# Position 7's native steps are spread over the steps of positions 2 and 3, with nine weight buffers and three shared sum tiles

## The chip, the cores and the metric

The kernel runs on one core of one Trainium2 chip. The metric is device time in microseconds (us). TensorE (PE in the profile) multiplies, PEld are its weight loads, VectorE (DVE) and ScalarE (ACT) do the elementwise work, SP issues the weight loads (DMAs), and each of these queues works in its own fixed order.

## The reference, cut to what matters

Two blocks on 256 tokens of width 1024: first a hybrid layer (state space and attention), then two layers of a conformer kind, the second with a mixture of experts. The change lies in that mixture, at the end of the program:

```
logits = xf @ w_router                      # 256 x 8 experts
top_vals, top_idx = top_k(logits, 2);  gates = softmax(top_vals)
# every expert e, on the tokens sent to it (d_ff = 3584):
y = (silu(x_e @ w1[e]) * (x_e @ w3[e])) @ w2[e] * gate
f = sum of y over each token's two experts
h = layer_norm(alpha * h + f + e_ple, ln2_g, ln2_b)
```

All is float32. Each expert has three weight matrices of 1024 x 3584, 44 MB in all, and all eight are read.

## The kernel before

The experts are sorted by their number of tokens into positions: position 0 is expert 0, and 1 to 7 hold the others, the largest first. Each position has a fixed number of token slots: 128 for 2 and 3, 128 and a further block of 64 (called NE) for 1, 64 for 0, 4 and 5, 32 for 6 and 7. Extra passes for experts that overflow stand behind branches at the end.

An expert's inner width of 3584 is cut into seven steps of 512 (NJ = 7). A step is six loads (units) of 1 MB: four for the up-projection (w1, w3), two for the down-projection (w2). `STEPS` lists the order in which the positions take steps; before, the end is `(1, 5, 6) * 7`, then `(2, 7) * 7`, then `(3,) * 7`, at indices 14 to 34, 35 to 48 and 49 to 55.

There are two kinds of steps. For positions 1, 2 and 3 (`WIDE`) each unit is split in two halves, and each half into a high part `whi`, which ScalarE casts (L305), and a low part `wlo`, which VectorE subtracts (L306); a product is then three matmuls on `whi`, `wlo` and the likewise split tokens (L324 to L326): 48 matmuls for an up-projection and 24 for a down-projection. These are called split steps here. For positions 0, 4, 5, 6 and 7 the raw weights are multiplied directly (native steps: L1583 up, L1612 down), without work for ScalarE and VectorE on the weights.

`passes` runs the loop: for step i it issues the up-projection (`hidden`), then the first half of the down-projection of step i-1 (`down`), then the transposes of step i's result (`later`), then the second half of that down-projection. Here this is called block i. When a position has finished its seventh step its sum is scaled by the gates (`scaled`, tiles `yh`, `yl`) and added to the tokens' rows `hb` one block later (`scatter`); for the last step `last_sums` does so. Positions 2 and 3 keep their sums in PSUM (two `sm` banks); those in `aside` (NE, 4, 5, 6, 7) keep them in an SBUF tile `y`, to which VectorE adds each step's product (L1632). A position's tokens are gathered into `xg` (split) or `xn` (native) shortly before its first step (`gather`).

Loads are issued by SP in order of use, in a ring of raw buffers, 8 KB per partition each: four in `rawp`, three in `raw2`, one in `raw4`, and two in `raw3` that are given up at step 2 (`narrow`), so eight from there on. Up to four units are prepared ahead (`rows_unit`, `ahead`), and the halves of three units are held at once. The order on each engine's queue is set by a scheduler when the program is built. Last, `rows` (called at a step index) builds two rows for the closing layer norm, and `last_norm` writes the result.

Of the kernel before, what the change touches and what calls it, by code (L numbers as in the profile page):

```python
# [8 lines left out]
F32 = mybir.dt.float32  # L9
# [8 lines left out]
P = 128  # L18
D = 1024
# [6 lines left out]
RAW3 = 2  # L26
# [9 lines left out]
NE = 8  # L36
FE = 3584
NJ = FE // 512
# [101 lines left out]
_, C_TRI, C_STRI, C_CAUS, C_SGN, C_IOTA, C_LESS = 0, 128, 256, 384, 512, 513, 641  # L140
# [62 lines left out]
def _steps(order):  # L203

    return [(e, order[:i].count(e)) for i, e in enumerate(order)]


def _moe_order(steps):


    out = []
    for i in range(len(steps) + 1):
        if i < len(steps):
            out += [(steps[i][0], 6 * steps[i][1] + t) for t in ((0, 2, 1, 3) if steps[i][0] in TURNS else range(4))]
        if i:
            out += [(steps[i - 1][0], 6 * steps[i - 1][1] + t) for t in (4, 5)]
    return out
# [2 lines left out]

TURNS = (0, 1, 4, 5, 6, 7)

STEPS = _steps((0, 0, 0, 4, 0, 4, 0, 4, 0, 4, 0, 4, 4, 4) + (1, 5, 6) * NJ + (2, 7) * NJ + (3,) * NJ)

WIDE = (1, 2, 3)

MORE = 5

WHOLE = [a + i for a in (0, 52) for i in (1, 2, 3, 4, 15, 16)]

FIXED = [e for e, _ in _moe_order(STEPS)].index(4)

# [16 lines left out]
class Kern:  # L249
    def __init__(self, tc, ctx, A, nring=(4, 3)):  # L250
# [14 lines left out]
        if "wm" in A:  # L265
            self.srcs += [(A["wm"][0, u], e in WIDE) for e, u in _moe_order(STEPS)[:FIXED]]

# [907 lines left out]
    def moe(self, l, h, hT, out):  # L1175
# [4 lines left out]
        tc, nc, A = self.tc, self.nc, self.A  # L1180
        mm = nc.tensor.matmul
        with ExitStack() as ctx:
            raw2 = ctx.enter_context(tc.tile_pool(name="raw2", bufs=3))
            mp = ctx.enter_context(tc.tile_pool(name="moe", bufs=1))
            self.gat = ctx.enter_context(tc.tile_pool(name="gat", bufs=1))
            self.xgs, self.xns, self.ohs = [], [self.gat] * 2, [self.gat] * 2

            rctx = ctx.enter_context(ExitStack())
            raw3 = rctx.enter_context(tc.tile_pool(name="raw3", bufs=RAW3))
            self.raws = [raw2] * 3 + [raw3] * RAW3 + self.raws  # L1190
            rctx2 = ctx.enter_context(ExitStack())
            rt = rctx2.enter_context(tc.tile_pool(name="rt", bufs=1))
            wrh, wrl = self.wr
# [67 lines left out]
            def choose(dst, src, ind, n):  # L1261
                nc.vector.tensor_mul(eq[:, :n], ind, src[:, None, :].to_broadcast([P, n, NE]))
                nc.vector.tensor_reduce(dst, eq[:, :n], axis=AX.X, op=OP.add)

            whof = rt.tile([P, NE + 1 + MORE], F32, name="whof")
            choose(whof[:, :NE], iota, perm, NE)
# [10 lines left out]
            nc.vector.tensor_tensor(ovf, ovf, caps, op=OP.is_gt)  # L1277
            nc.vector.tensor_reduce(whof[:, NE + MORE:], ovf, axis=AX.X, op=OP.add)
            order = rt.tile([P, NE + 1], F32, name="order")
            choose(order[:, :NE], ovf[:, :NE], self.less, NE)  # L1280
            nc.vector.tensor_reduce(order[:, NE:], ovf[:, :NE], axis=AX.X, op=OP.add)
            ind = rt.tile([P, MORE, NE + 1], F32, name="ind")
            for i in range(MORE):
                nc.vector.scalar_tensor_tensor(ind[:, i], order, float(i), ovf, op0=OP.is_equal, op1=OP.mult)

            def overflowing(dst, src):
# [3 lines left out]
                if dst[1] is not None:  # L1290
                    nc.vector.tensor_sub(some, some, dst[1])
                each = rt.tile([P, MORE, NE + 1], F32, name="each", bufs=2)
                nc.vector.tensor_mul(each, ind, some[:, None, :].to_broadcast([P, MORE, NE + 1]))
                nc.vector.tensor_reduce(dst[0], each, axis=AX.X, op=OP.add)
# [23 lines left out]
            self.raws = [raw4] + self.raws  # L1318
            self.ahead = 3
            self.mp = ctx.enter_context(tc.tile_pool(name="exp", bufs=1, side="right"))  # L1320
            self.xgs, self.xns, self.ohs = [], [self.gat] * 2, [self.gat] * 2

            def narrow():
                self.raws = [p for p in self.raws if p is not raw3]
# [1 line left out]
            def widen():  # L1326
# [7 lines left out]
            self.srcs += [(A["wm"][0, u] if e == 0 else self.wsrc(es[e - 1], u), e in WIDE)  # L1334
                          for e, u in _moe_order(STEPS)[FIXED:]]
            a, b, q = P, P // 2, P // 4
            fin, stats, gb = [], [], []

            def rows():

                for i in range(2):
                    t = self.ya.tile([P, D], F32, name=f"y{5 + i}")
                    for c in range(2):
                        acc = self.bank([P, 4, P], "acc")
                        for k in range(4):
                            at = KD * i + 4 * c + k
                            mm(acc[:, k], self.gb[:, at:at + 1].to_broadcast([P, P]), self.ident, start=True, stop=True)
                        nc.scalar.copy(t[:, 512 * c:512 * c + 512], acc.rearrange("p a b -> p (a b)"))
                    gb.append(t)
                fin.extend(self.ya.tile([P, D], F32, name=n) for n in ("y7", "y8"))  # L1350
                stats.append(self.mp.tile([P, NT, 2, 6], F32, name="stats"))

            def done(sums):
                self.last_norm(r, sums, fin, stats[0], *gb, out)
            self.passes(posp, gatep, STEPS, r, first, [
                {4: [(4, b)]}, {1: [(1, a), (NE, b)], 5: [(5, b)]},
                {6: [(6, q)], 7: [(7, q)]}, {2: [(2, a)]}, {3: [(3, a)]}], (NE, 4, 5, 6, 7), {2: narrow, 3: widen, len(STEPS) - NJ + 2: rows}, done)
            n = nc.values_load(who[0:1, NE + MORE:], min_val=0, max_val=MORE)
            with ExitStack() as some:
                for i in range(MORE):  # L1360
                    some.enter_context(tc.If(n > i))
                    e = nc.sync.value_load(who[0:1, NE + i:NE + i + 1], min_val=0, max_val=NE - 1)
# [97 lines left out]
    def passes(self, pos, gate, steps, r, got, groups, aside=(), events={}, done=None):  # L1460

        todo, left, ys = None, None, {}
        groups = list(groups)
        for i, step in enumerate(steps + [None]):
            new = None
            if i in events:
                events[i]()

            for e, _ in steps[i:i + (3 if i > 5 else 1)]:
                if e not in got:  # L1470
                    got.update(self.gather(gate, groups[0], self.one_hot(pos, groups.pop(0))))
            later = None
            if step:
                e, j = step
                out, later = self.hidden([b[1] for b in got[e]], e in TURNS)
                new = (e, j, out)
            if left:
                self.scatter(left, r)
                left = None
            if not step:  # L1480
                break
            if todo:
                e, j, gs = todo
                if j == 0:
                    ys[e] = [self.ya.tile([P, D], F32, name=f"y{7 if b[0] == 4 else b[0]}") if b[0] in aside else
                             [self.bank([P, 512], "sm") for _ in range(2)] for b in got[e]]
                    ys[e] = [[y[:, :512], y[:, 512:]] if b[0] in aside else y for y, b in zip(ys[e], got[e])]
                here = [b[0] in aside for b in got[e]]
                self.down(ys[e], gs, j, here, (0,))
                later()  # L1490
                self.down(ys[e], gs, j, here, (1,))
                if j == NJ - 1:
                    left = self.scaled(ys[e], got[e])
            else:
                later()
            todo = new
        done(self.last_sums(r, todo, ys, got, aside))
# [180 lines left out]
```

## Time and profile before

| what | us |
|---|---|
| median of 3 runs (lowest, highest) | 1919.47 (1915.2, 1926.11) |
| the profiled execution | 1920.03 |
| its span, first to last instruction | 1918.2 |
| TensorE busy in the span | 1799.3 (94%) |
| VectorE, ScalarE busy | 1156.7 (60%), 845.3 (44%) |
| granted clock of TensorE, mean | 0.977 |

The shares are means over stages with different limits; the span alone doesn't say which engine a stage waits for. The stretches that the change touches are the table's rows from 1549 us to the end: positions 2 and 7 from there to about 1780, position 3 from there to 1900, and the closing norm in the last 18 us.

### The profile page before, as it was taken

The numbers are of one execution on the slowest core, as the hardware profiler recorded it, in microseconds if no ns is written. First come the engines' busy times: TensorE is split into PE (matmuls) and PEld (weight loads), VectorE is DVE, ScalarE is ACT, GpSimd is POOL, SyncE is SP. The second block draws the span as 40 slices with busy tenths as digits, with TensorE's granted clock in tenths as the row PEclk, the third lists the DMA queues.
The fourth block names the chain that finished last, engine by engine and source line by source line (L and its number), as shares of the span: only waits on it lengthen the run. The fifth ranks groups of instructions, "written<-read, shape, count | busy, mean of one in ns | idle before, by whom it ended". The sixth has DMA issues, their size and how long they took to land.

```text
span 1918.2 us, 26708 instructions
## 1 busy us (share of the span) xinstructions
PE 1799.3 (94%) x10242; PEld 1289.8 (67%) x10242; DVE 1156.7 (60%) x2109; ACT 845.3 (44%) x1369; POOL 8.8 (0%) x21
## 2 busy tenths in 40 slices
PE   6999999998998999999799889999999989899996
PEld 6998888897875999887554234444444546656775
DVE  6548899757897655589840014334444465647887
ACT  4756566444473545347411013322333444535674
POOL 0000000000000000000000000000000000000000
PEclk9999999999998999999889999999999999999998
DMA  6543444454534554463449999789999999999992
GB/s 246 195 150 116 154 160 170 168 191 173 218 110 156 187 196 176 175 237 133 162 190 420 421 421 418 318 352 381 384 382 383 371 382 405 421 421 421 353 339 85
DMA packets 82873, 515.17 MB, mean 269 GB/s; under 512 B 8688, under 2 KB 17568, under 8 KB 22960
## 3 DMA queue, kind: packets, MB, share of 16 engines
q1 hardware_dynamic: 69296, 494.57, 65.4%
q10 hardware_dynamic: 13440, 18.80, 3.1%
q8 instruction: 83, 1.36, 0.3%
q14 instruction: 54, 0.44, 0.1%
HBM read 512.24 MB, written 1.10 MB: 268 GB/s over the span
## 4 chain that ended last, share of the span: by engine, by line
PE 79%; DVE 11%; DMA 5%; ACT 2%; issue 2%; DVEq 0%; ACTq 0%
PE acc L325 14%; PE acc L326 14%; PE acc L324 14%; PE acc L1583 12%; DMA raw<-in_wm 5%; DVE wlo L306 4%; PE sm L1612 3%; PE sm L325 3%; PE sm L326 3%; PE sm L324 2%; DVE cv L1024 2%; PE acc L1612 2%; PE tp L1554 1%; ACT whi L305 1%; PE acc L358 1%
## 5 line engine op out<-in xcount | busy, mean ns | idle before, releaser
L306 DVE TENSOR_TENSOR wlo<-raw,whi 128x1024 fp32r<-128x1024 f32 x490 | 583.1, 1219 | 216.7 <-ACT whi L305 215.9
L305 ACT CAST whi<-raw 128x1024 fp32r<-128x1024 f32 x490 | 494.9, 1048 | 170.9 <-PE acc L326 70.7
L1583 PE MATMUL acc<-raw,xn 128*64 128x512 f32 (+1 forms) x1344 | 276.9, 602 | 15.0 <-DMA raw<-in_wm 15.0
L1583 PEld LDWEIGHTS acc<-raw,xn 128*64 128x64 f32 (+1 forms) x1344 | 82.3, 129 | 184.7 <-issue 155.9
L1544 ACT ACTIVATE eg<-acc 128x512 f32<-128x512 f32 x63 | 37.6, 597 | 361.2 <-PE acc L1583 293.3
L324 PE MATMUL acc<-uhi,whi 128*128 128x272 f32 (+1 forms) x576 | 168.4, 293 | 1.4 <-DVE rs_t L382 1.4
L325 PE MATMUL acc<-ulo,whi 128*128 128x272 f32 (+1 forms) x576 | 167.9, 292 | 0.0
L326 PE MATMUL acc<-uhi,wlo 128*128 128x272 f32 (+1 forms) x576 | 166.5, 289 | 0.0
L324 PE MATMUL acc<-hhi,whi 128*128 128x256 f32 x544 | 152.5, 280 | 0.0
L325 PE MATMUL acc<-hlo,whi 128*128 128x256 f32 x544 | 152.2, 280 | 0.0
L326 PE MATMUL acc<-hhi,wlo 128*128 128x256 f32 x544 | 151.7, 279 | 0.0
L325 PE MATMUL acc<-wlo,xg 128*128 128x512 f32 x336 | 135.7, 404 | 6.2 <-DVE wlo L306 6.2
L324 PE MATMUL acc<-whi,xg 128*128 128x512 f32 x336 | 134.5, 400 | 2.3 <-ACT whi L305 2.3
L326 PE MATMUL acc<-whi,xg 128*128 128x512 f32 x336 | 133.9, 399 | 0.0
L324 PEld LDWEIGHTS acc<-uhi,whi 128*128 128x128 f32 x576 | 109.7, 191 | 4.6 <-issue 2.7
L325 PEld LDWEIGHTS acc<-ulo,whi 128*128 128x128 f32 x576 | 109.6, 190 | 1.4 <-issue 1.0
L326 PEld LDWEIGHTS acc<-uhi,wlo 128*128 128x128 f32 x576 | 109.6, 190 | 1.2 <-issue 1.1
L1024 DVE SCALAR_TENSOR_TENSOR cv<-u,cols,cv 128x256 f32<-128x256 f32 x240 | 102.0, 477 | 2.1 <-ACT cv L1022 1.3
L324 PEld LDWEIGHTS acc<-hhi,whi 128*128 128x128 f32 x544 | 102.3, 188 | 0.2
L325 PEld LDWEIGHTS acc<-hlo,whi 128*128 128x128 f32 x544 | 102.1, 188 | 0.1
L326 PEld LDWEIGHTS acc<-hhi,wlo 128*128 128x128 f32 x544 | 101.8, 187 | 0.0
L1612 PE MATMUL sm<-raw,g 128*64 128x512 f32 (+1 forms) x392 | 90.7, 600 | 0.0
(516 smaller groups left out, 2957.6 us busy)
## 6 DMA issues: line engine op xcount, KB each, us to landing
raw<-in_wm SPq DMA_DIRECT2D x336, 1024.0 KB, 10.4
raw<-in_ws SPq DMA_DIRECT2D x131, 1024.0 KB, 4.8
row<-in_rows ACTq DMA_DIRECT2D x9, 512.0 KB, 4.4
seg<-racs ACTq DMA_DIRECT2D x8, 512.0 KB, 4.1
rb<-in_rpb ACTq DMA_DIRECT2D x8, 512.0 KB, 3.4
ck<-rnck ACTq DMA_DIRECT2D x4, 544.0 KB, 5.6
x<-in_x SPq DMA_DIRECT2D x2, 512.0 KB, 5.2
gn<-in_rows ACTq DMA_DIRECT2D x4, 256.0 KB, 3.3
```

What stands on the lines that cost most here:

```text
L305: nc.scalar.copy(hi, x)
L306: nc.vector.tensor_sub(lo, x, hi.bitcast(F32))
L324: nc.tensor.matmul(out, lhi, rhi, start=start, stop=False)
L325: nc.tensor.matmul(out, lhi, rlo, start=False, stop=False)
L326: nc.tensor.matmul(out, llo, rhi, start=False, stop=stop)
L358: self.nc.tensor.matmul(outs[tb], x[2][:, kk, s], w.raw[:, k], start=start, stop=stop)
L1024: nc.vector.scalar_tensor_tensor(cv[:, m], u[:, m, t:t + T], w, cv[:, m], op0=OP.mult, op1=OP.add)
L1544: nc.scalar.activation(t, h[0], AF.Copy if len(h) == 1 else AF.Silu)
L1554: i = nc.tensor.transpose(tp[:, k], h[0][:, k * P:k * P + P], self.ident)
L1583: self.nc.tensor.matmul(h[0][at:at + n], x[0][:, k0 + k + q], w.raw[:, k + q], start=k0 + k == 0, stop=k0 + k + m == KD)
L1612: self.nc.tensor.matmul(out[h:h + s], x[0][:, kx], w.raw[:, k], start=first and k < m, stop=last and k >= n - m)
```

## The change

`STEPS` ends now in `(1, 5, 6) * 7`, then `2, 7`, three times `2, 2, 7`, three times `3, 3, 7`, and `3`; the steps are the same, 56 in number. `raw2` has four buffers instead of three, so the ring holds nine from step 3 on. To make room, the sums of 4 and 6, of 5 and one norm row, and of NE and 7 share the tiles `ya`, `yb`, `yc` (`SUMS`); the first pool holds one `xn` tile instead of two; and the result's rows (`fin`) take turns in the `xg` tiles. `rows` is called at index 52 instead of 51.

```
-STEPS = _steps((0, 0, 0, 4, 0, 4, 0, 4, 0, 4, 0, 4, 4, 4) + (1, 5, 6) * NJ + (2, 7) * NJ + (3,) * NJ)
+STEPS = _steps((0, 0, 0, 4, 0, 4, 0, 4, 0, 4, 0, 4, 4, 4) + (1, 5, 6) * NJ + (2, 7) + (2, 2, 7) * 3 + (3, 3, 7) * 3 + (3,))
...
+SUMS = {2: "b", 4: "a", 5: "b", 6: "a", 7: "c", NE: "c"}
...
-            raw2 = ctx.enter_context(tc.tile_pool(name="raw2", bufs=3))
+            raw2 = ctx.enter_context(tc.tile_pool(name="raw2", bufs=4))
...
-            self.xgs, self.xns, self.ohs = [], [self.gat] * 2, [self.gat] * 2
+            self.xgs, self.xns, self.ohs = [], [self.gat], [self.gat] * 2
...
-            self.raws = [raw2] * 3 + [raw3] * RAW3 + self.raws
+            self.raws = [raw2] * 4 + [raw3] * RAW3 + self.raws
...
-                    t = self.ya.tile([P, D], F32, name=f"y{5 + i}")
+                    t = self.ya.tile([P, D], F32, name="y" + "ab"[i])
...
-                fin.extend(self.ya.tile([P, D], F32, name=n) for n in ("y7", "y8"))
+                fin.extend(self.turn_of(self.xgs, [P, D], "xg", F32) for _ in range(2))
...
-  {2: narrow, 3: widen, len(STEPS) - NJ + 2: rows}
+  {2: narrow, 3: widen, len(STEPS) - 4: rows}
...
-  ys[e] = [self.ya.tile([P, D], F32, name=f"y{7 if b[0] == 4 else b[0]}") if b[0] in aside else
+  ys[e] = [self.ya.tile([P, D], F32, name="y" + SUMS[b[0]]) if b[0] in aside else
```

The new program's lines from L222 on are two higher than before (L324 is L326). Three places of the two orders follow, before first.

TensorE's queue where a split up-projection of position 2 ends and position 7's down-projection (`sm` and `acc` from `raw`, with the transposes `tp` between) follows:

```order
L326 MATMUL acc<-whi,xg 128x512
L1612 MATMUL sm<-raw,g_14281 32x512 x4
L1554 MATMUL tp<-cst,eg 128x128 x4
L1612 MATMUL acc<-raw,g_14281 32x512 x4
L1583 MATMUL acc<-raw,xn 32x512 x16
L324 MATMUL sm<-whi,egs 128x512
```

```order
L1614 MATMUL sm<-raw,g_14025 32x512 x4
L1556 MATMUL tp<-cst,eg 128x128 x4
L1614 MATMUL acc<-raw,g_14025 32x512 x4
L326 MATMUL acc<-whi,xg 128x512
L327 MATMUL acc<-wlo,xg 128x512
```

Behind the native down-projection stood the native up-projection of 7's next step, which uses raw weights; now the up-projection of position 2's next step stands there, whose third row needs a `wlo`.

VectorE's queue around the same place (`eg` is the product of the two gate halves, `egs` the low part of the transposed result, `y_13772` and `yc` the sum of position 7, `g` its gate):

```order
L1551 TENSOR_TENSOR eg<-eg,acc 128x512
L1632 TENSOR_TENSOR y_13772<-y_13772,sm 128x512
L362 TENSOR_TENSOR egs<-tp,egs 128x512
L1632 TENSOR_TENSOR y_13772<-y_13772,acc 128x512
L306 TENSOR_TENSOR wlo<-raw,whi 128x1024 x4
L1597 TENSOR_REDUCE g_14282<-tp 128x256
```

```order
L1553 TENSOR_TENSOR eg<-eg,acc 128x512
L1634 TENSOR_TENSOR yc<-yc,sm 128x512
L364 TENSOR_TENSOR egs<-tp,egs 128x512
L1634 TENSOR_TENSOR yc<-yc,acc 128x512
L308 TENSOR_TENSOR wlo<-raw,whi 128x1024 x10
L1553 TENSOR_TENSOR eg<-eg,acc 128x512
```

Four halves followed the second addition, for the down-projection after a native up-projection; now ten follow it, eight for the split up-projection that is TensorE's next block and two for the down-projection after it.

VectorE's queue at the end of the last block, before the closing norm (`yl` is the low part of a scaled sum, `hb` the tokens' rows):

```order
L306 TENSOR_TENSOR wlo<-raw,whi 128x1024 x2
L362 TENSOR_TENSOR egs<-tp,egs 128x512
L306 TENSOR_TENSOR wlo<-raw,whi 128x1024 x4
L1643 SCALAR_TENSOR_TENSOR yl<-sm,gsl,yh 128x512
L1512 TENSOR_TENSOR hb<-hb,acc 128x512 x2
```

```order
L1634 TENSOR_TENSOR yc<-yc,acc 128x512
L1645 SCALAR_TENSOR_TENSOR yl<-yc,gsl,yh 128x512 x2
L1658 TENSOR_TENSOR hb<-hb,acc 128x512 x2
L308 TENSOR_TENSOR wlo<-raw,whi 128x1024 x2
L1658 TENSOR_TENSOR hb<-hb,acc 128x512
L308 TENSOR_TENSOR wlo<-raw,whi 128x1024 x2
L1658 TENSOR_TENSOR hb<-hb,acc 128x512
L1645 SCALAR_TENSOR_TENSOR yl<-sm,gsl,yh 128x512
```

The last four halves (the last down-projection's weights) stood behind `egs` alone; now they stand behind position 7's last addition, its scaling and its first scatter. On SP one more expert load, the eighth, stands ahead of the reading of `who`, the router's result.

## Rows read from the trace of the kernel before

**Rows 1.** The page's forty slices: busy share of the DMA engines, in tenths.

```profile
DMA  6543444454534554463449999789999999999992
```

**Rows 2.** Table by stretch: length, busy us (instructions) by engine, clock, DMA share, GB/s.

```profile
1048.00:1131.00 83.00, 69.15 (x296) 23.39 (x293) 4.86 (x9) 5.49 (x11) 0.00 (x0) 1.00 1.01 421
1260.00:1500.00 240.00, 233.00 (x1134) 108.90 (x1133) 100.89 (x117) 77.58 (x101) 0.00 (x0) 1.00 0.92 379
1584.88:1614.00 29.12, 26.69 (x129) 17.68 (x128) 16.22 (x17) 14.72 (x19) 0.00 (x0) 0.88 1.00 394
1614.00:1641.89 27.89, 25.45 (x129) 16.63 (x128) 17.20 (x19) 13.27 (x17) 0.00 (x0) 0.94 1.01 422
...
1805.88:1897.00 91.12, 91.12 (x399) 72.15 (x398) 76.70 (x72) 64.54 (x73) 0.00 (x0) 1.00 0.71 266
...
1779.73:1805.90 26.17, 25.10 (x119) 20.44 (x119) 22.44 (x24) 17.09 (x21) 0.00 (x0) 0.93 0.95 365
```

**Rows 3.** TensorE's timeline, blocks of 2 and 7: start, us, instruction, [idle before].

```profile
1598.74 3.62 PE L1583 MATMUL acc<-raw,xn 128*32 128x512 f32 x32
1604.04 0.50 PE L324 MATMUL sm<-whi,egs 128*128 128x512 f32 x1 [1.68 <-ACT whi L305]
1605.30 0.80 PE L325 MATMUL sm<-wlo,egs 128*128 128x512 f32 x1 [0.76 <-DVE wlo L306]
...
1614.01 0.39 PE L324 MATMUL acc<-whi,xg 128*128 128x512 f32 x1
...
1627.88 3.62 PE L1583 MATMUL acc<-raw,xn 128*32 128x512 f32 x32
...
1634.43 0.50 PE L325 MATMUL sm<-wlo,egs 128*128 128x512 f32 x1 [0.76 <-DVE wlo L306]
...
1641.89 0.40 PE L324 MATMUL acc<-whi,xg 128*128 128x512 f32 x1
```

**Rows 4.** ScalarE's timeline after a native up-projection.

```profile
1631.59 0.60 ACT L1544 ACTIVATE eg<-acc 128x512 f32<-128x512 f32 x1 [3.90 <-PE acc L1583]
1632.08 5.77 ACT L305 CAST whi<-raw 128x1024 fp32r<-128x1024 f32 x6
```

**Rows 5.** TensorE's timeline: first products of two blocks of position 3.

```profile
1858.15 0.39 PE L324 MATMUL acc<-whi,xg 128*128 128x512 f32 x1
...
1875.63 0.40 PE L324 MATMUL acc<-whi,xg 128*128 128x512 f32 x1
```

**Rows 6.** TensorE's timeline where position 3 follows the last step of 7.

```profile
1777.43 1.07 PE L1612 MATMUL acc<-raw,g 128*32 128x512 f32 x8
1779.73 0.50 PE L324 MATMUL acc<-whi,xg 128*128 128x512 f32 x1 [1.23 <-ACT whi L305]
1781.30 0.50 PE L325 MATMUL acc<-wlo,xg 128*128 128x512 f32 x1 [1.06 <-DVE wlo L306]
```

**Rows 7.** VectorE's timeline at the same place.

```profile
1778.77 0.68 DVE L1632 TENSOR_TENSOR y<-y,acc 128x512 f32<-128x512 f32 x1
1779.36 0.74 DVE L1643 SCALAR_TENSOR_TENSOR yl<-y,gsl,yh 128x512 fp32r<-128x512 f32 x1
1780.03 2.35 DVE L306 TENSOR_TENSOR wlo<-raw,whi 128x1024 fp32r<-128x1024 f32 x2
```

**Rows 8.** Timelines of VectorE and TensorE near the end.

```profile
1892.06 4.63 DVE L306 TENSOR_TENSOR wlo<-raw,whi 128x1024 fp32r<-128x1024 f32 x4 [0.26 <-ACT whi L305]
...
1899.51 0.40 PE L326 MATMUL sm<-whi,egs 128*128 128x512 f32 x1
```

**Rows 9.** SP's queue from 986 to 1000 us: loads behind the router's result.

```profile
987.55 12.32 SPq L298 DMA_DIRECT2D raw<-in_wm  x4
```

**Rows 10.** Timelines of TensorE and ScalarE: the gather for position 2, the norm rows.

```profile
1514.40 0.67 PE L1433 MATMUL acc<-oh,thi 128*128 128x128 f32 x4
1515.10 3.57 ACT L1438 CAST xg<-acc 128x256 fp32r<-128x256 f32 x8 [1.16 <-PE acc L1433]
...
1802.22 3.29 PE L1347 MATMUL acc<-cst,wr 128*128 128x128 f32 x28
```

More of the change, by code (lines that the diff above doesn't have):

```diff
@@ L1320, in moe @@
             self.mp = ctx.enter_context(tc.tile_pool(name="exp", bufs=1, side="right"))
-            self.xgs, self.xns, self.ohs = [], [self.gat] * 2, [self.gat] * 2
+            self.xgs, self.xns, self.ohs = [], [self.gat], [self.gat] * 2
             def narrow():
@@ L1356, in moe @@
                 {4: [(4, b)]}, {1: [(1, a), (NE, b)], 5: [(5, b)]},
-                {6: [(6, q)], 7: [(7, q)]}, {2: [(2, a)]}, {3: [(3, a)]}], (NE, 4, 5, 6, 7), {2: narrow, 3: widen, len(STEPS) - NJ + 2: rows}, done)
+                {6: [(6, q)], 7: [(7, q)]}, {2: [(2, a)]}, {3: [(3, a)]}], (NE, 4, 5, 6, 7), {2: narrow, 3: widen, len(STEPS) - 4: rows}, done)
             n = nc.values_load(who[0:1, NE + MORE:], min_val=0, max_val=MORE)
```

## The prediction

> **What bounds the kernel now.** I read the page's forty slices first. The loads' share of time stands at 3 to 6 tenths until slice 21 and at 7 to 9 from slice 22 (1007 us) to the last but one: there the kernel streams expert weights [rows 1]. Then a table by stretch, which shows three regimes [rows 2]. While positions 1, 5 and 6 take turns (1260 to 1500) TensorE is busy 233.00 of 240 us and the loads 0.92: TensorE is the bound, narrowly. While 2 and 7 alternate (a pair is 1614.00 to 1641.89) the loads stand at 1.01 and 422 GB/s and TensorE has 2.4 us to spare: the loads are the bound. In the last steps of position 3 TensorE is busy 91.12 of 91.12 us and the loads fall to 0.71. So the change moves cheap TensorE work out of a stretch that is short of loads into one that is short of TensorE. One load is 1.0486 MB; at 421 GB/s that is 2.49 us, a step of six 14.94 us, wherever loads bind.
>
> Third, TensorE's timeline, to price a step. I cut it into blocks as the loop issues them: up-projection of step i, then down-projection of step i-1.
> - Split after native (A): 1614.01 to 1627.88, 13.87 us [rows 3].
> - Native after split (C): 1627.88 to 1641.89, 14.01 us. In it TensorE stops after 32 native products, until the first `whi` (1.68) and then the first `wlo` (0.76) of the next weights are there [rows 3]. ScalarE shows why: its cast of the native result (1631.59) stands ahead of the casts that make `whi` (from 1632.08), so these can't start while the native products run [rows 4].
> - Split after split (B): 1858.15 to 1875.63, 17.48 us, without a wait [rows 5].
>
> A pair A + C has 27.9 us of TensorE with its waits against 29.9 us of loads; an all-split step has 17.5 against 14.9. Spread evenly, the 21 steps of 2, 7 and 3 would need 21 x 14.94 = 314 us of loads and nothing more; the question is what TensorE needs for them in the new order.
>
> **The change part by part.** Steps 37 to 54 become six triples: split, split, native, that is A, B, C. Their work is the same products as before; what counts is where TensorE stands still.
>
> *The new seam.* Between the two split steps of a triple, native down-projection ends, and the next split up-projection follows at once (before, a native up-projection stood there, which needs no split). VectorE's queue now has, behind the second addition into `yc`, all ten `wlo` that follow; the first of them is the one that the next TensorE block starts with. The addition needs the down-projection's last product. So each triple gets a wait: addition, then one `wlo`. Before there is one such place, where 7 is followed by 3 [rows 6, 7]: the native down-projection is issued at 1777.43, the addition runs at 1778.77 for 0.68, a `yl` at 1779.36 for 0.74, the first `wlo` from 1780.03, and TensorE waits 1.23 and then 1.06, 2.29 in all. Without the `yl` (about 0.65 in steady state) the `wlo` ends near 1780.6 and TensorE is some 2.0 us late against an unbroken run. In the first triple the addition is a copy on ScalarE ahead of the casts; I add 0.9 there. Bounds: 0, if the addition came early enough, and 2.9. I take 2.0. Queued behind the waiting `wlo` are the other nine; TensorE uses one half of a load in six products of 0.235 (17.48 over 72 products and four transposes), 1.4 us, and VectorE makes one in 1.16 (4.63 for four), so the delay doesn't grow [rows 5, 8].
>
> *A triple* is then 13.87 + 17.48 + 2.0 + 14.01 = 47.4 us; six are 284.2. Its eighteen loads need 44.9: TensorE, with its waits, becomes the bound, by 2.5 us. The loads' slack lies in the ninth buffer.
>
> *Ninth weight buffer.* One more load is issued ahead of SP's wait for the router's result: eight in that group instead of seven. Before, that load waited until 987.55 [rows 9]; the stretch after it is bound by loads (share 1.01 from 1048 to 1131, TensorE 69 of 83 us) [rows 2], so it shifts by one load: -2.5 us, and the stage of 1, 5, 6 starts that much earlier. Bounds 0 (the buffer comes free no earlier) and -5 (two loads). In that stage TensorE is the bound and the buffer is worth nothing.
>
> *Three sum tiles, one `xn` fewer in the old pool, output rows in the `xg` tiles.* No operation is added. The users of one tile lie far apart: 4 ends before 6 begins, the block NE of position 1 ends before 7 begins, 2's `xg` is unread long before the output. What would cost is a wait of a first write for the last read; there are blocks between each pair. 0.
>
> *Moved work that loses its cover.* Position 3's gather lay in the stretch bound by loads. A gather whose eight copies ScalarE made in one go (3.57 us, from 0.7 after TensorE's start) took TensorE 4.3 us [rows 10]. Now ScalarE has four `whi` (5.77 for six, so 0.96 each [rows 4]) between those copies, and TensorE can be some copies ahead (an estimate, 1.1): 4.3 + 3.8 - 1.1 = 7, of which 2 replace that triple's wait: +5 (2.3, if the `whi` cost nothing, to 8). Position 2's scatter, eight products of 0.235, lies in a triple: +1.9. The norm rows' 32 products, 28 of them in 3.29: +3.7 [rows 10].
>
> *The end.* Position 7 now ends one step before the last, so its sum is scattered just ahead of the last down-projection. VectorE's order there after the last native product: addition 0.68, two `yl` 1.48, two additions into `hb` of the same form 1.36, then four `wlo` (4.63) with another (0.68) between, then TensorE's six products (1.4) and four scatter products (0.95): 11.2, with hand-overs between the engines 12. Bounds: 8.5 if TensorE's 24 + 4 + 8 products run unbroken, 14.
>
> *The sum.* The block at 1584.88 is the first of triple one; before and after are the same up to there but for the -2.5: 1582.4. Plus 284.2 + 0.9 (triples), + 5 + 1.9 + 3.7, + 13.87 (block 55, split after native), + 12: 1904.0. Before, the last down-projection product started at 1899.51 [rows 8] and ended 0.23 later; what follows it is the same. Difference +4.2 us. The profiled execution took 1920.03 us (span 1918.2); the median of the three runs is 1919.47, 0.56 below it. So 1920.03 + 4.2 - 0.56 = 1923.7: I forecast **1924 us, no measurable change**, half a per cent (9.6 us) being about what a measurement of this kernel tells from none.
>
> **TensorE's clock.** In the pairs the granted clock is 0.94, in the first of them 0.88; in the stretch of 1, 5, 6 and in the last steps of 3 it is 1.00 [rows 2]. It fell to its low level (1.2 GHz) after the native step and its wait, and matmuls ran at 0.80 and 0.50 then [rows 3]. C as priced contains one such fall; the C from 1598.74 to 1614.01, with twice the time at the low level, took 15.27, 1.26 more. Without any fall the 24 products and transposes after the wait would take 6.2 instead of 7.5, so a triple 1.2 less. [...]
>
> **The rivals.**
> A. *The loads bind: faster.* The waits overlap with the slack that the interleaving gives, and a triple takes 44.9 us, the time of its loads. Then 6 x 2.5 = 15 us less, 1909 us. For it: 1.01 in all pairs, and the same steps of 3 without any wait in rows 5. Against it: both waits come from the order in the queues, and rows 3, 6 show them while loads were landed or not. 0.2.
> B. *The clock falls twice per triple: slower.* At the seam TensorE does 2.4 us of thin native products, waits 2, and starts a block of 48 dense ones. At the one such place before (1779.73) the clock of the stretch that follows is 0.93 [rows 2]. A fall cost 1.26 above; six, at 1.5 for blocks that are denser, are +9: 1933 us. It decides if TensorE's granted clock in triples is under about 0.93. 0.25.
> C. *The buffer and order do less than they say*: the eighth early load waits as long as before, so the shift of 2.5 us fails, and nothing else changes: 1926. 0.05. The forecast itself, triples of 46 to 48 us, has 0.5.
>
> **How the numbers follow.** The forecast's own range: a triple without a fall of the clock, -7, to a gather at 8 and a tail at 14, +5: 1917 to 1929. Faster by over 0.5% (under 1909.9) is A: 0.2. Slower (over 1929.1) is B and some of the forecast's upper edge: 0.3. Within: 0.5. The low end of the range is A with two early loads and the cheap gather (1909 - 2.5 - 2.7 = 1903.8, taken as 1903), the high end B with the dear gather and tail (1933 + 3 + 2 = 1938).
>
> **What would show it.** (1) At six places, after native down-projection, TensorE waits about 2 us for `wlo`, VectorE's addition into `yc` just ahead; if those waits are under 0.5 us, the seam step is wrong. (2) Triples of 46 to 48 us, with the loads' share 0.93 to 0.98, not 1.01; a share of 1.01 with 44.9 is rival A. (3) The granted clock in the triples: 0.96 is the forecast, below 0.93 rival B. (4) The load at 987.55 issued by 980, and the stage of 1, 5, 6 earlier by 2.5 us. (5) Between the last native product and the last down-projection product 12 us. The forecast is wrong as a whole if triples differ from 47.4 by more than 1.6 us.

## The result, and the profile after

The changed kernel took 1932.94 us (median of 15 runs, 1927.77 to 1943.25), the kernel before 1918.1 us in 15 runs of the same series: 1.0081 of it, 95% interval 1.0067 to 1.0095. It is slower by 0.8%, 15 us. The forecast of 1924 us is 9 us short. The time lies in the whole range that was stated (1903 to 1938) but above the forecast's own (1917 to 1929), and "no measurable change" was wrong. The profiled execution took 1936.5 us; some 5 us of it are a delay ahead of 100 us that e1 and e4 don't have.

A table by stretch of the changed kernel (length, busy us (instructions) by engine, granted clock, DMA share, GB/s): its six triples, each from one split block behind a native one to the next, and the end.

```profile
1590.41:1638.47 48.06, 43.21 (x206) 30.16 (x204) 31.14 (x31) 27.12 (x33) 0.00 (x0) 0.96 0.97 372
1638.47:1685.95 47.48, 43.41 (x205) 30.36 (x204) 32.28 (x33) 25.97 (x31) 0.00 (x0) 0.96 0.98 399
1685.95:1740.69 54.74, 50.56 (x246) 37.15 (x244) 32.96 (x35) 27.83 (x39) 0.00 (x0) 0.91 0.90 358
1740.69:1788.73 48.04, 43.97 (x214) 30.59 (x212) 36.09 (x38) 28.24 (x33) 0.00 (x0) 1.00 0.98 379
1788.73:1842.47 53.74, 49.72 (x238) 34.28 (x237) 32.35 (x33) 28.31 (x35) 0.00 (x0) 0.97 0.98 395
1842.47:1889.99 47.52, 43.45 (x206) 30.31 (x204) 32.32 (x33) 25.97 (x31) 0.00 (x0) 0.96 0.90 347
1889.99:1915.60 25.61, 23.82 (x106) 16.22 (x105) 19.64 (x24) 11.14 (x15) 0.00 (x0) 1.00 0.15 64
```

The plain triples (second, sixth) take 47.5 us. The third holds position 3's gather, the fourth position 2's scatter, the fifth the norm rows. In none is TensorE busy for the whole time, and in none are the loads at the 1.01 that they had in the pairs [rows 2]: neither is the bound, the waits between the engines are. The list of TensorE's waits (engine, line waited for: us in total, times, longest) for 1590.4 to 1916 names them:

```profile
PE sm L326 <- ACT whi L307: 10.0, 6, 1.7
PE sm L327 <- DVE wlo L308: 5.3, 7, 0.8
PE acc L327 <- DVE wlo L308: 4.8, 5, 1.0
PE acc L326 <- ACT whi L307: 4.1, 5, 1.6
```

The first two are in the main the wait behind each native up-projection, known from [rows 3]; the last two stand at the new seam, in five triples (in the third the gather stands there). TensorE's timeline there (start, us, instruction, [idle before]):

```profile
1651.45 1.06 PE L1614 MATMUL acc<-raw,g 128*32 128x512 f32 x8
1653.14 0.49 PE L326 MATMUL acc<-whi,xg 128*128 128x512 f32 x1 [0.62 <-ACT whi L307]
1654.65 0.80 PE L327 MATMUL acc<-wlo,xg 128*128 128x512 f32 x1 [1.02 <-DVE wlo L308]
```

And the queues of ScalarE and VectorE at the same place:

```profile
1644.76 1.99 ACT L307 CAST whi<-raw 128x1024 fp32r<-128x1024 f32 x2
1651.56 0.58 ACT L363 CAST egs<-tp 128x512 fp32r<-128x512 f32 x1 [4.81 <-PE tp L1556]
1652.04 5.79 ACT L307 CAST whi<-raw 128x1024 fp32r<-128x1024 f32 x6
```

```profile
1651.00 0.69 DVE L1634 TENSOR_TENSOR yc<-yc,sm 128x512 f32<-128x512 f32 x1 [0.34 <-PE sm L1614]
1652.18 0.69 DVE L364 TENSOR_TENSOR egs<-tp,egs 128x512 fp32r<-128x512 f32 x1 [0.49 <-ACT egs L363]
1652.79 0.68 DVE L1634 TENSOR_TENSOR yc<-yc,acc 128x512 f32<-128x512 f32 x1
1653.38 6.89 DVE L308 TENSOR_TENSOR wlo<-raw,whi 128x1024 fp32r<-128x1024 f32 x6
```

ScalarE stands still for 4.81 us, because the cast of the split result (`egs`), which needs the transposes, is ahead of the `whi` in its queue; the six casts behind it then run without a wait for a load. VectorE has both additions and its part of `egs` ahead of the first `wlo`. So there are two queue orders at the seam, of which the prediction named VectorE's alone.

A third sort of row is the clock. A native block with its wait in the first triple, the part behind that wait in the fifth, the stretch behind the second triple's seam, and the two split blocks of the second and of the fifth triple:

```profile
1625.99:1638.47 12.48, 10.04 (x62) 5.94 (x61) 7.19 (x7) 8.15 (x10) 0.00 (x0) 1.00 0.95 381
1834.00:1842.40 8.40, 7.63 (x28) 5.92 (x28) 6.91 (x7) 6.25 (x8) 0.00 (x0) 0.80 1.01 412
1653.14:1657.81 4.67, 3.65 (x9) 2.67 (x10) 4.67 (x5) 4.67 (x5) 0.00 (x0) 0.66 1.02 412
1638.47:1673.49 35.02, 33.38 (x145) 24.41 (x143) 25.12 (x26) 17.84 (x21) 0.00 (x0) 0.95 1.01 412
1788.73:1822.23 33.50, 31.87 (x146) 23.23 (x144) 25.12 (x26) 17.84 (x21) 0.00 (x0) 1.00 1.01 421
```

In the first, second and sixth triple the clock falls to its low level once, behind the seam; in the fifth once, behind the native step; in the gather's triple at both places; in the fourth (1.00) not at all. The two split blocks took 35.02 us with a fall and 33.50 without one, so a fall costs 1.5.

### The profile page after: what moved, and what is told of

It reads as the page before. It is cut to its first block, busy times and chain, and to the rows that moved or that the text cites. A ratio compares the mean times of both kernels' runs of the same rounds, so it can differ in the third digit from the quotient of the medians.

```text
span 1934.7 us, 26712 instructions
## 1 busy us (share of the span) xinstructions
PE 1804.6 (93%) x10242; PEld 1292.4 (67%) x10242; DVE 1156.8 (60%) x2109; ACT 844.2 (44%) x1369; POOL 8.8 (0%) x21
## 5 line engine op out<-in xcount | busy, mean ns | idle before, releaser
L326 PE MATMUL acc<-uhi,whi 128*128 128x272 f32 (+1 forms) x576 | 168.8, 293 | 1.3 <-DVE rs_t L384 1.3
L326 PE MATMUL acc<-hhi,whi 128*128 128x256 f32 x544 | 153.1, 281 | 0.0
L326 PE MATMUL acc<-whi,xg 128*128 128x512 f32 x336 | 136.9, 408 | 5.7 <-ACT whi L307 5.2
L328 PE MATMUL acc<-whi,xg 128*128 128x512 f32 x336 | 136.0, 405 | 0.0
L326 PEld LDWEIGHTS acc<-uhi,whi 128*128 128x128 f32 x576 | 110.3, 192 | 4.5 <-issue 2.4
L326 PEld LDWEIGHTS acc<-hhi,whi 128*128 128x128 f32 x544 | 102.3, 188 | 0.2
```

What stands on the lines that cost most here:

```text
L326: nc.tensor.matmul(out, lhi, rhi, start=start, stop=False)
L328: nc.tensor.matmul(out, llo, rhi, start=False, stop=stop)
```

## The experiments

The theory: the changed kernel's loss lies in its triples, where ScalarE's and VectorE's queues put work that waits for TensorE ahead of casts for which TensorE waits. Its rivals: the loads and their ring, the ninth buffer or the shared tiles, and chance in the profiled executions.

**e1, buffers and tiles alone.**

```
-STEPS ... + (2, 7) + (2, 2, 7) * 3 + (3, 3, 7) * 3 + (3,))
+STEPS ... + (2, 7) * NJ + (3,) * NJ)
...
-len(STEPS) - 4: rows
+len(STEPS) - NJ + 2: rows
```

> The changed kernel with the old order of steps (2 and 7 in turn, then 3): only the ninth buffer, the shared tiles and one xn tile fewer are left of the change. Theory 1 (the order of the steps costs the time, through TensorE's waits at its seams): 1 to 2.5 us less than before, about 1916. Theory 2 (the tiles or the buffer cost what the changed kernel's trace shows before 100 us, where it is 5 us late): 1921 to 1924, with the same 5 us early in its trace. Theory 3 (that early delay is chance): as theory 1, and no delay of 5 us before 100 us in this trace.

1916.29 us against 1917.41: ratio 0.9998 (0.9984 to 1.0012). TensorE waits for loads for 13.0 us between 990 and 1140 us against 13.8 before. The buffer and the tiles cost nothing and bring nothing that can be measured. The 5 us ahead of 100 us that the changed kernel's trace shows are not here: chance.

**e2, the order alone.**

```
-raw2 = ctx.enter_context(tc.tile_pool(name="raw2", bufs=4))
+raw2 = ctx.enter_context(tc.tile_pool(name="raw2", bufs=3))
```

> The changed kernel with three buffers in raw2 instead of four: the new order of steps with the old ring of eight. Theory 1: triples of 47.5 us as in the changed kernel, since TensorE's waits and not the loads set them; 1 to 2 us above the changed kernel, about 1934. Theory 2 (the ring): triples of 48.5 us or more, 1940 and above, since loads now bind.

1937.94 us, ratio 1.0115 (1.0096 to 1.0134); plain triples 47.5 us. With the eight buffers it is as slow as the change, or slightly slower; its tiles are those of e1, which cost nothing. So the order of the steps is the cause.

**e3, the first casts ahead of the others.** `behind` opens a scope in which what is issued on ScalarE (0) or VectorE (1) stands behind the cast of the unit with the given number among the next ones, from step 36 on; no operation is added. The main edits:

```
-nc.scalar.activation(t, h[0], AF.Copy if len(h) == 1 else AF.Silu)
+with self.behind(1, (0,) if len(h) == 1 else ()):    # behind the second next unit's whi
+    nc.scalar.activation(t, h[0], AF.Copy if len(h) == 1 else AF.Silu)
...
-self.split(gh, gl, tp)
+with self.behind(0, (0, 1) if self.native else ()):  # behind the next unit's whi and wlo
+    self.split(gh, gl, tp)
...
-nc.vector.tensor_add(y[c], y[c], o[c])
+with self.behind(0, (1,)):                           # behind the next unit's wlo
+    nc.vector.tensor_add(y[c], y[c], o[c])
```

> The changed kernel, but from step 36 on ScalarE's queue has the whi casts of the next split units ahead of the cast of a native result (eg) and of the split result's high part (egs), and VectorE's queue has the first wlo ahead of position 7's additions and of egs; no operation is added or removed. Theory 1 (both waits per triple are an order in these queues: 2.4 us after the native step, 1.7 at the seam): the waits go, triples fall to 44.9 us, where the loads bind (share 1.0), and the triple with the norm rows and the one with the gather lose 5 us or more; 1933 - 6 x 2.6 - 5 = 1912, 1908 to 1918. Theory 2 (the weights were not there in time, the loads or their halves): the waits stay at some 4 us per triple, 1930 to 1935. Of the clock: if its falls follow the waits, the mean granted clock of the triples rises from 0.96 to 0.99 or more; if they follow the thin native products, it stays at 0.96.

1896.65 us, ratio 0.9891 (0.9873 to 0.9909): 21 us below the kernel before and 34 below the changed one (e4). Theory 1, by 11 us more than its range. Its triples by stretch, in order, and the end:

```profile
1581.25:1622.45 41.20, 41.20 (x205) 29.11 (x204) 31.16 (x31) 27.32 (x33) 0.00 (x0) 1.00 1.01 422
1622.45:1664.30 41.85, 41.48 (x205) 29.14 (x204) 32.27 (x33) 25.87 (x30) 0.00 (x0) 1.00 1.01 420
1664.30:1717.12 52.82, 50.98 (x245) 37.98 (x244) 32.88 (x34) 28.98 (x40) 0.00 (x0) 0.90 0.98 405
...
1760.94:1809.32 48.38, 47.77 (x237) 33.10 (x236) 32.18 (x33) 28.24 (x35) 0.00 (x0) 1.00 1.01 421
1809.32:1850.55 41.23, 41.23 (x205) 29.14 (x204) 32.19 (x33) 25.99 (x31) 0.00 (x0) 1.00 1.01 420
1850.55:1876.10 25.55, 23.75 (x106) 16.18 (x105) 20.04 (x24) 11.58 (x14) 0.00 (x0) 1.00 0.31 127
```

A plain triple takes 41.2 to 41.9 us, TensorE busy for all but 0.4 of it at most, without a fall of the clock: the falls of the changed kernel's plain triples went with the waits. That is below the 44.9 of its loads, which I had taken for a floor: the loads run at 1.01 (0.98 in the gather's triple), and the ring's lead pays the difference. ScalarE and VectorE at its second seam show the queues turned round:

```profile
1631.24 1.99 ACT L308 CAST whi<-raw 128x1024 fp32r<-128x1024 f32 x2 [0.51 <-DMA raw<-in_wm]
1635.54 0.59 ACT L371 CAST egs<-tp 128x512 fp32r<-128x512 f32 x1 [2.31 <-PE tp L1567]
```

```profile
1634.57 2.35 DVE L308 TENSOR_TENSOR wlo<-raw,whi 128x1024 fp32r<-128x1024 f32 x2
1636.84 0.68 DVE L1648 TENSOR_TENSOR yc<-yc,sm 128x512 f32<-128x512 f32 x1
```

**e4, the changed kernel again** (no edit).

> The changed kernel once more, for a second trace of it. Theory 1: 1933, the stretch from triple one to the last down-projection product again 325 us long against 315 before, with one fall of the clock in each triple, at the seam or after the native step; and no delay of 5 us before 100 us (chance). Theory 2: the 5 us before 100 us are there again.

1931.08 us, ratio 1.0078 (1.0059 to 1.0097). From triple one to the end of the last down-projection (1581.83 to 1906.93) it took 325.1 us, against 325.0 in the first trace (1590.41 to 1915.37); the early 5 us are absent.

**e5 and e6, the two halves of e3.** e5 has the first of e3's three changes, e6 the other two (and the like for the first step's copies).

> The changed kernel with only one half of e3's edit: ScalarE's cast of a native result stands behind the whi casts of the next two split units; the seam keeps its queue order. Theory 1 (two separate queue orders): the wait after the native step (1.68 and 0.76 us) goes, the seam's (0.62 and 1.02, six times) stays; the triple loses 2.4 to 2.8 us, 44.7 to 45.1, so with the cheaper norm rows 1912 to 1918. If a clock fall follows each wait, one fall of about 1.4 us is left in each triple, now always at the seam. Theory 2 (the seam alone costs what the change lost): hardly faster than the changed kernel, 1926 or more.

> The other half of e3's edit alone: the first casts ahead of position 7's additions and of egs; the wait after the native step stays. Theory 1: the wait at the seam goes (1.64) and the fall of the clock behind it, which comes back after the native step in each triple: the triple loses 2.0 to 3.5 us, 44.0 to 45.5, 1910 to 1918. Theory 2 (the seam alone costs what the change lost): nearly all of e3's gain, 1898 to 1903.

e5: 1909.11 us, ratio 0.994 (0.9921 to 0.9958). e6: 1920.65, 0.9997 (0.9984 to 1.001). The expected times missed, e5 by 3 us below its range, e6 by 3 above; the plain triples came as theory 1 of each expected. The second and last triple of e5:

```profile
1628.97:1673.72 44.75, 43.12 (x205) 30.28 (x204) 32.35 (x33) 25.98 (x31) 0.00 (x0) 0.96 1.01 421
1820.06:1864.81 44.75, 43.11 (x206) 30.28 (x204) 32.35 (x33) 25.97 (x31) 0.00 (x0) 0.96 0.95 363
```

and of e6:

```profile
1633.43:1677.42 43.99, 41.56 (x206) 29.14 (x205) 32.12 (x33) 26.00 (x31) 0.00 (x0) 1.00 1.01 421
1831.85:1875.86 44.01, 41.57 (x206) 29.14 (x205) 32.14 (x33) 25.98 (x31) 0.00 (x0) 1.00 0.94 377
```

From 47.5, e5 takes 2.75 and e6 3.5, so in plain triples the seam weighs more, by the fall of the clock that goes with it: the native wait alone leaves the clock at 1.00 there (it does fall in e6's fourth and fifth triple, 0.96 and 0.97). Over the six triples it is the other way: 299.6 us in the changed kernel, 279.8 in e5, 286.4 in e6, 269.3 in e3. e5 also shortens the triples of the gather and the norm rows (50.3 and 50.4 us; in e6 55.0 and 51.7).

**e7, both halves in the old order of steps.**

```
-STEPS ... + (2, 7) + (2, 2, 7) * 3 + (3, 3, 7) * 3 + (3,))
+STEPS ... + (2, 7) * NJ + (3,) * NJ)
...
-len(STEPS) - 4: rows
+len(STEPS) - NJ + 2: rows
```

> Both halves of e3's edit with the old order of steps (2 and 7 in turn, then 3) and the nine buffers of e1. Theory 1 (the pairs are bound by their loads, share 1.01, so their waits hide): within 3 us of e1, 1912 to 1917, and so the new order is worth 15 us or more once its waits are gone. Theory 2 (the queue order alone makes e3's gain, in any order of steps): 1900 or less.

1909.7 us, ratio 0.9943 (0.9923 to 0.9963), between the theories. From one native block to the next the pairs took 23.6 and 23.5 us while the ring's lead lasted, then 29.5, 31.3 and 30.5, against 29.9 for their twelve loads. In these TensorE waits for loads, and for casts for which ScalarE itself stands waiting for a load (1628.32):

```profile
PE sm L334 <- ACT whi L308: 5.2, 4, 1.7
PE acc L1597 <- DMA raw<-in_wm: 4.9, 5, 1.4
```

```profile
1628.32 1.99 ACT L308 CAST whi<-raw 128x1024 fp32r<-128x1024 f32 x2 [7.55 <-DMA raw<-in_wm]
```

So a DMA share of 1.01 did not mean that TensorE was held by the loads in the first pairs, and did in the later ones. With the casts first, the new order is worth about half a per cent, 10 us (0.9891 of the kernel before in e3, 0.9943 in e7); with the casts as they were it costs 15.

**e8, another order with the casts first.**

```
-STEPS ... + (2, 7) + (2, 2, 7) * 3 + (3, 3, 7) * 3 + (3,))
+STEPS ... + (2, 7) * 3 + (2,) * 4 + (3,) * 3 + (7, 3) * 4)
```

> Both halves of e3's edit and another order of the last 21 steps: 2, 7 three times, 2 four times, 3 three times, then 7, 3 four times, so that the all-split run, in which TensorE falls behind the loads, stands in the middle, and pairs, in which it catches up, at the end. TensorE's own time from the start of the stretch to the last down-projection is worked out to 284 us (7 blocks of 14.0, 6 of 9.7, 6 of 17.5, gather 5, norm rows 4, scatter 2, end 12), e3's took 294; the 19 steps' loads take 284. Theory 1 (after e3 the loads bind in the stretch, and their lead is lost at the end, where the last load lands 18 us before the last product): 1884 to 1892. Theory 2 (the order of steps no longer matters once the waits are gone): 1895 to 1898.

1908.25 us, ratio 0.9937 (0.9918 to 0.9956). Both expectations missed. The pairs outrun the loads by the third (that native up-projection takes 6.86 instead of 3.62 us, with waits for loads), then the all-split run lets the loads' share fall to 0.89 between 1700 and 1760 us. My sum had TensorE's time and the loads' time each in total, and neither in order: the ring's lead is too short for seven steps of one kind.

**e9, the kernel before again** (no edit).

> The kernel before once more, for a second trace of it: how much of the difference of 14 us between the medians (the stretch from triple one to the last down-projection product shows 10.4 of it) is chance of the one execution that was profiled before. Theory 1 (its stretch there was some 3 us longer than usual, by its falls of the clock): the same stretch, 314.9 us in the first trace, takes 310 to 313 here. Theory 2 (the rest lies ahead of the stretch): 314 to 316.

One run, 1914.87 us; theory 1, by 1 us more than its range. The stretch of [rows 2] from 1584.88 to the end of the last down-projection, in the first trace and then in this one:

```profile
1584.88:1899.74 314.86, 296.84 (x1411) 210.55 (x1410) 218.08 (x222) 175.40 (x211) 0.00 (x0) 0.96 0.91 365
```

```profile
1585.77:1894.69 308.92, 290.13 (x1411) 205.14 (x1410) 218.04 (x222) 175.69 (x211) 0.00 (x0) 0.99 0.91 373
```

The same work took 5.9 us less, with the clock at 0.99 instead of 0.96: the trace that the prediction was made from had more falls than this one. e1, which has the same order of steps, took 311.1. The difference to the changed kernel's 325.0 is 10.1 by the first trace and 16.0 by the second; the medians' 14.8 lies between.

**e10, the casts first from step 14 on.**

```
-self.late = done and 36 <= i < len(STEPS) - 1
+self.late = done and 14 <= i < len(STEPS) - 1
```

> e3's edit, from step 14 on instead of step 36: in the stretch of positions 1, 5 and 6 too the first casts stand ahead of the native results' casts and of the additions. Theory 1 (TensorE is the bound there, and its 13 us of waits for whi and wlo between 1131 and 1581 us are such queue orders): 5 to 12 us below e3, 1885 to 1892. Theory 2 (position 1's waits have another cause, or the loads and the later casts take their place): within 3 us of e3, 1894 to 1900.

1887.67 us, ratio 0.9838 (0.9817 to 0.9859): theory 1. TensorE's waits for casts from 1131 us to 1581 in e3 were these, 10.0 us and not the 13 of the expectation:

```profile
PE acc L335 <- DVE wlo L308: 5.1, 7, 1.1
PE sm L335 <- DVE wlo L308: 3.8, 5, 0.8
...
PE acc L334 <- ACT whi L308: 1.1, 2, 0.8
```

In e10 1.8 us of such waits are left between 1131 and 1880.

**e11, the gather and the norm rows moved.**

```
-for e, _ in steps[i:i + (3 if i > 5 else 1)]:
+for e, _ in steps[i:i + (2 if i > 40 else 3 if i > 5 else 1)]:
...
-len(STEPS) - 4: rows
+len(STEPS) - 3: rows
```

> e3 with two more steps moved: position 3's gather is issued one step later (among the split products of the block before its first step, instead of in one piece at a seam), and the norm rows' 32 products one step later (among split products instead of native ones). Theory 1 (both cost more in the changed kernel than was forecast because of what they stand in: the gather's triple took 11.6 us more than the others in e3, the norm rows' triple 7.2): 3 to 8 us below e3, 1888 to 1893, the gather's excess 6 to 9, the norm rows' 4 to 5. Theory 2 (their cost is their own products and copies, wherever they stand): within 2 us of e3.

1893.83 us, ratio 0.9872 (0.9849 to 0.9895), 3 below e3 in the medians, with intervals that overlap. Its third, fifth and sixth triple:

```profile
1662.60:1708.15 45.55, 45.55 (x246) 33.85 (x244) 32.52 (x34) 29.67 (x40) 0.00 (x0) 1.00 1.01 421
...
1752.05:1800.61 48.56, 44.48 (x206) 31.04 (x205) 32.34 (x33) 26.94 (x32) 0.00 (x0) 0.93 1.02 421
1800.61:1847.42 46.81, 45.10 (x237) 32.84 (x236) 32.27 (x33) 28.04 (x35) 0.00 (x0) 1.00 1.01 420
```

The gather's triple falls from 52.8 to 45.6, without a wait and with the clock at 1.00. The norm rows became dearer: 95.4 us for the last two triples against 89.6 in e3, for two reasons. In the fifth triple the native block has lost the row products, and TensorE waits 3.3 us for a `whi` that ScalarE could not cast before its load came, with a fall of the clock (0.93):

```profile
1790.27 1.99 ACT L308 CAST whi<-raw 128x1024 fp32r<-128x1024 f32 x2 [8.19 <-DMA raw<-in_wm]
```

In the sixth it waits 1.7 us for ScalarE's copy of a norm row. So the loads took back part of what the gather had given.

**e12, e10 with the gather of e11.**

> e10 with the gather's part of e11: the first casts ahead of the others from step 14 on, and position 3's gather one step later; the norm rows stay where e10 has them. Theory 1 (the gather's triple gives the 7 us that it gave in e11, since the last load still lands 17 us ahead of the last product in e10, so the loads' lead has room for it): 1879 to 1883. Theory 2 (the loads, at a share of 1.01 in the whole stretch, take the gain back as waits): 1885 to 1889.

1884.29 us (1882.35 to 1887.51), ratio 0.9816 (0.9791 to 0.984). The median lies between the two expectations; the trace speaks for the first, its gather's triple taking 45.5 us, and TensorE waits for no load in the six triples:

```profile
1657.94:1703.48 45.54, 45.54 (x246) 33.84 (x244) 32.50 (x34) 29.51 (x40) 0.00 (x0) 1.00 1.01 421
```

It beats both kernels: 36 us below the kernel before (1920.39 in that series), 1.8%. Against e10 the intervals overlap.

## Why the prediction was right and wrong

The sum was right in the triple's size and wrong in the ninth buffer and in the moved work. The change is measurable: what came is the "slower" to which the forecast gave 0.3.

- *The triple.* Priced at 47.4 us, measured 47.5, with one fall of the clock as priced (0.96). The seam's wait was put at 2.0 us: TensorE waits 0.62 and 1.02, and two split blocks without a fall took 33.50 us in the fifth triple against 31.5 in e3 (1622.45 to 1653.97), 2.0 more. The size was right; the cause was half of it, since ScalarE's queue has its own share, and the 1.23 of [rows 6], put down to VectorE, was such a wait for `whi`. In part the triple's fit is luck: the 14.01 us of C hold a fall behind the native step, but in the plain triples that block took 12.5 us without one, and the fall came at the seam.
- *The ninth buffer: failed.* Forecast -2.5, measured 0 (e1, within 0.2%). The load that had waited until 987.55 [rows 9] was issued at 973.9 in e1, as forecast, but TensorE's waits for loads fell only by 0.8 us. The load after it was issued at 988.5, where the one before it had waited until then; why the one load of lead is not worth its 2.5 us no run shows.
- *Gather and norm rows: mis-sized.* Forecast +5 and +3.7; against the plain triples +7.2 and +6.2. The gather breaks off dense work; the block behind it ran at the low clock for some of its products, and a second fall stands behind that triple's native step (0.91). The 1.1 us that TensorE was to be ahead of the copies stand in no row. The norm rows were hoisted among thin native products. These took 3.64 us alone and 9.9 with the 32 row products between them.
- *The scatter* was sized rightly: forecast +1.9, and the fourth triple's two split blocks (1740.69 to 1776.25) took 35.56 us against 33.50 in the fifth, both without a fall, 2.1 more. That its triple is only 0.5 above the plain ones is the fall that it lacks. With the first triple's copies (0.9 forecast, 0.6 measured) these four make 3 us more than the sum, counted against the plain triples.
- *The end.* 12 us forecast from the last native product to the last down-projection product, 11.4 measured.
- *The base.* The sum was made against one execution whose stretch took 314.9 us; the same kernel took 308.9 in the second. By the stretch alone the forecast (321.6) was 3.4 short of 325.0. The buffer's 2.5 and these 3.4 leave some 3 of the 9 us by which 1924 missed; they fit a base that was some 3 us too long, as far as the traces bound it, but that share is not measured by itself.
- *Rival A* (loads bind, 44.9 per triple) didn't come; e3 shows that it needed the waits gone, and that the loads are not a floor for a triple while the ring has a lead. *Rival B* gave the time, 1933, without its mechanism: it wanted two falls of the clock per triple and a granted clock below 0.93, and there was one, at 0.96; only the gather's triple had two. *Rival C* was right that the buffer gives nothing, but not in its reason: the load did come early.

## What to carry to other kernels

Before reordering steps, read what stands ahead of each cast or copy in its engine's queue at the new neighbours: here an order that put a result's cast before the next weights' cost more than the balance of loads gave, and turning that order round was worth 34 us without an operation less. A load share of 1.01 says that loads run, not that TensorE waits for them; the list of waits says that, and where it names a cast, read what the cast waited for (in e7 and e11 a load). A ring can lend its lead for a few steps. Where the granted clock falls now and then, one trace is a base with an error of several us: take a second one before adding up small terms.

## What the runs showed that I had not expected

- The clock does not fall for each wait. With both waits in a plain triple (47.5 us) it fell once, at the seam. With the seam's alone (e5) it fell in the second and sixth triple (0.96) and not in the first, fourth and fifth (1.00); with the native step's alone (e6) in the fourth and fifth and not in the first, second and sixth; with neither (e3) in none of these. The gather's triple fell in every one of these kernels. The Trainium skill (TensorE: Matmul & The Clock Gate, "HAM oscillation — how this bites in real kernels") describes bursts of matmuls that each start at the reduced clock because the wait for a load ahead of each is long enough. Here the longer wait was not the one that counted: in the changed kernel's plain triples the native step's 2.4 us (1.67 and 0.76) left the clock up, and the seam's 1.6 (0.62 and 1.02) brought it down. What decides between them no run shows.
- Six triples ran in 269.3 us in e3, while their 108 loads at 2.49 us are 269: the loads ran nearly all the time, TensorE was busy for 266.4 us of it, and a plain triple was still 3.7 us shorter than its loads. In e12 the six took 262.8 us, so even over six triples the loads' time was no floor.
